# Eight-expert feed-forward: the last w2 load recut, the last result cut at column 320, three stores in halves

## The chip, the core and the metric

The kernel runs on one core of a Trainium2 chip. The metric is the device time of one execution in microseconds (us); lower is better. Engines that matter here: PE (TensorE, matrix products), ACT (ScalarE) and DVE (VectorE), which empty the accumulators, POOL (GpSimd), whose queue issues all weight loads, and SP (SyncE), whose queue issues most stores. Sixteen DMA engines carry all loads and stores of the core.

## What is computed

```python
n_experts, capacity, hidden, expert_hidden = 8, 256, 512, 2048
h = np.matmul(x, w1) + b1[:, np.newaxis, :]
h = np.maximum(h, 0)
return (np.matmul(h, w2) + b2[:, np.newaxis, :]).astype(np.float32)
```

All inputs and the output are float32 in HBM. An expert has a w1 of 512 x 2048 and a w2 of 2048 x 512, 4 MB each; the eight experts' weights are 64 MB of the 71.4 MB that are read. The output is 4 MB.

## The kernel before, in words

Weights and most of x are cast to float16 by the load itself, which POOL's queue issues (`load_w1` L69, `load_w2` L75, `load_x` L63). So a load reads 4 MB of float32 and writes 2 MB of float16 into SBUF. Products are float16 with float32 accumulators.

w2 of an expert is laid out as 128 partitions by 16 rows of 512 columns ("row" below means one of these 16; row j of every partition together is a contraction step of 128). Experts 0 to 5 load w2 whole, expert 6 in two halves of 8 rows, and the last, expert 7, in six pieces with a tile each (L85 to L91): rows 0-4, 4-8, 8-12, 12-14 with all columns, then rows 14-16 as two pieces of 256 columns. In one partition a piece of whole rows is one contiguous run, so one DMA packet; a piece of two rows by 256 columns is two packets of 512 B.

`first_product(e)` (L105) makes the hidden layer: 16 groups of 4 matmuls, each emptied by ACT with bias and ReLU (L117). Halfway it puts the next expert's transposes of x (L97). `second_product(e)` (L139) multiplies hidden by w2: it opens the accumulators with a matmul of the bias row (L151) and then walks the pieces of w2 in the order in which they are loaded (L163), 32 matmuls of 512 columns. Expert 7 has two column blocks, 0-256 and 256-512, with two accumulators each (one per 128 tokens), so 64 matmuls of 256 columns. When a block has its last row, `store` (L127) copies one accumulator by DVE (L130) and the other by ACT (L131) to SBUF and issues the store: from SP, one DMA of 512 KB for experts 0 to 6 (L137); for each block of expert 7 one DMA of 128 KB from SP (L134) and one from ACT (L135).

Steps run s = 0 to 10: first product of expert s, then second product of expert s - 3 (LAG). The order of instructions on PE and on POOL's queue is that of the program (`ordered`). POOL's order of loads is a list (L207 to L214): x, w1 and w2 in the order of use, w2 three experts behind w1. A load of POOL waits until its tile is free (three buffers each for w1 and w2; each piece of expert 7 has its own), and until the load eight places earlier on the queue has landed, because eight completion semaphores are used in turn.

Of the kernel before, what the change touches and what calls it, by code (L numbers as in the profile page):

```python
# [11 lines left out]
def kernel(  # L12
# [9 lines left out]
    nc = tc.nc  # L22
    fp32 = mybir.dt.float32
    fp16 = mybir.dt.float16
    E, T, H = x.shape
    M = w1.shape[2]
    P = 128
    nTB = T // P
    nKC = H // P
    nJ = M // P  # L30
    HH = H // 2
    LAG = 3
    nXF32 = 2

    def ordered(ins):
        return tc.keep_in_program_order(ins)

    singles = ctx.enter_context(tc.tile_pool(name="singles", bufs=1))
    w1_pool = ctx.enter_context(tc.tile_pool(name="w1", bufs=3))
    w2_pool = ctx.enter_context(tc.tile_pool(name="w2", bufs=3))  # L40
    w2t_pool = ctx.enter_context(tc.tile_pool(name="w2t", bufs=1))
    x_pool = ctx.enter_context(tc.tile_pool(name="xp", bufs=4))
    xT_pool = ctx.enter_context(tc.tile_pool(name="xTp", bufs=2))
    hT_pool = ctx.enter_context(tc.tile_pool(name="hT", bufs=LAG + 2))
    out_pool = ctx.enter_context(tc.tile_pool(name="outp", bufs=2))
    psum_x = ctx.enter_context(tc.tile_pool(name="psum_x", bufs=1, space=bass.MemoryType.PSUM))
    psum_h = ctx.enter_context(tc.tile_pool(name="psum_h", bufs=3, space=bass.MemoryType.PSUM))
    psum_o = ctx.enter_context(tc.tile_pool(name="psum_o", bufs=2, space=bass.MemoryType.PSUM))
# [10 lines left out]
    w1_sb = [None] * E  # L59
    w2_sb = [None] * E  # L60
# [14 lines left out]
    def load_w2(e):  # L75
        src = w2[e].rearrange("(p j) h -> p j h", j=nJ)
        w2_sb[e] = []
        if e < E - 1:
            t = w2_pool.tile([P, nJ, H], fp16, tag="w2", name="w2sb")
            step = nJ if e < E - 2 else nJ // 2  # L80
            for lo in range(0, nJ, step):
                ordered(nc.gpsimd.dma_start(out=t[:, lo : lo + step, :], in_=src[:, lo : lo + step, :]))  # L82
                w2_sb[e].append((lo, lo + step, 0, H, t[:, lo : lo + step, :]))
            return
        for lo, hi, c0, c1 in (  # L85
            (0, 4, 0, H), (4, 8, 0, H), (8, 12, 0, H), (12, 14, 0, H),
            (14, 16, 0, HH), (14, 16, HH, H),
        ):
            t = w2t_pool.tile([P, hi - lo, c1 - c0], fp16, tag=f"w2_{lo}_{c0}", name=f"w2_{lo}_{c0}")
            ordered(nc.gpsimd.dma_start(out=t, in_=src[:, lo:hi, c0:c1]))  # L90
            w2_sb[e].append((lo, hi, c0, c1, t))  # L91

    def transposes(e):
        pt = psum_x.tile([P, nKC, T], fp16, tag="psx", name="psx")
# [10 lines left out]
    def first_product(e):  # L105
        hT[e] = hT_pool.tile([P, nJ, T], fp16, tag="hT", name="hT")
        for j in range(nJ):
            ph = psum_h.tile([P, T], fp32, tag="ph", name="ph")
            for kc in range(nKC):
                ordered(nc.tensor.matmul(  # L110
                    out=ph,
                    lhsT=w1_sb[e][:, kc, :].rearrange("p (q j) -> p q j", j=nJ)[:, :, j],
                    rhs=xT[e][:, kc, :],
                    start=(kc == 0),
                    stop=(kc == nKC - 1),
                ))
            nc.scalar.activation(  # L117
                out=hT[e][:, j, :],
                in_=ph,
                func=mybir.ActivationFunctionType.Relu,  # L120
                bias=b1T[:, j, e : e + 1],
                scale=1.0,
            )
            if j == nJ // 2 and e + 1 < E:
                transposes(e + 1)

    def store(e, po, c0, c1, split):  # L127
        w = c1 - c0
        out_sb = out_pool.tile([P, nTB, w], fp32, tag=f"out{w}", name=f"out{w}")
        nc.vector.tensor_copy(out=out_sb[:, 0, :], in_=po[0])  # L130
        nc.scalar.copy(out=out_sb[:, 1, :], in_=po[1])  # L131
        dst = out[e].rearrange("(p tb) h -> p tb h", tb=nTB)[:, :, c0:c1]
        if split:
            nc.sync.dma_start(out=dst[:, 0, :], in_=out_sb[:, 0, :])  # L134
            nc.scalar.dma_start(out=dst[:, 1, :], in_=out_sb[:, 1, :])  # L135
        else:
            nc.sync.dma_start(out=dst, in_=out_sb)  # L137

    def second_product(e):  # L139
        if e < E - 1:  # L140
            blocks = [(0, H, psum_o, "po")]
        else:
            blocks = [(0, HH, psum_o, "po"), (HH, H, psum_h, "ph")]
        acc = {}
        for c0, c1, pool, tag in blocks:
            for tb in range(nTB):
                t = pool.tile(
                    [P, c1 - c0], fp32, tag=tag if tag == "ph" else f"{tag}{tb}", name=f"acc{tb}"
                )
                acc[c0, tb] = t  # L150
                ordered(nc.tensor.matmul(  # L151
                    out=t,
                    lhsT=ones1,
                    rhs=b2_sb[0:1, e * H + c0 : e * H + c1],
                    start=True,
                    stop=False,
                ))
        for lo, hi, p0, p1, t in w2_sb[e]:
            mine = [b for b in blocks if p0 <= b[0] and b[1] <= p1]
            for tb in range(nTB):  # L160
                for j in range(lo, hi):
                    for c0, c1, _, _ in mine:
                        ordered(nc.tensor.matmul(  # L163
                            out=acc[c0, tb],
                            lhsT=hT[e][:, j, tb * P : (tb + 1) * P],
                            rhs=t[:, j - lo, c0 - p0 : c1 - p0],
                            start=False,
                            stop=(j == nJ - 1),
                        ))
            if hi == nJ:  # L170
                for c0, c1, _, _ in mine:
                    store(e, [acc[c0, tb] for tb in range(nTB)], c0, c1, e == E - 1)

    x32 = singles.tile([P, nXF32, nTB, H], fp32)
    for e in range(nXF32):
# [4 lines left out]
        out=b2_sb,  # L180
        in_=b2.rearrange("e h -> (e h)").rearrange("(o f) -> o f", o=1),
# [10 lines left out]
    for j in range(nJ):  # L192
        for s in range(2):
            ordered(nc.tensor.matmul(  # L194
                out=pb[s * 64 : (s + 1) * 64, j, :, :],
# [5 lines left out]
    for s in range(2):  # L201
        nc.vector.tensor_copy(  # L202
            out=b1T[s * 64 : (s + 1) * 64, :, :], in_=pb[s * 64 : (s + 1) * 64, :, :, s]
        )
    transposes(0)

    loads = []  # L207
    for s in range(1, E + LAG):
        if s < E:
            if s >= nXF32:  # L210
                loads.append((load_x, s))
            loads.append((load_w1, s))
        if s >= LAG:
            loads.append((load_w2, s - LAG))  # L214
    n = 0

    def issue_until(done):
        nonlocal n
        while n < len(loads) and not done():
            loads[n][0](loads[n][1])  # L220
            n += 1

    for s in range(E + LAG):
        issue_until(lambda: (
            (min(s + 2, E - 1) < E and w1_sb[min(s + 2, E - 1)] is not None)
            and (s + 2 < LAG or w2_sb[min(s + 2 - LAG, E - 1)] is not None)
        ))
        if s < E:
            first_product(s)
        if s >= LAG:  # L230
            second_product(s - LAG)


# [28 lines left out]
```

## Time and profile before

| what | value |
|---|---|
| median of 5 runs | 185.97 us (185.74 to 186.18) |
| profiled execution, own time | 185.97 us |
| its span, first to last instruction | 184.0 us |
| PE busy | 139.4 us (76%) |
| ACT busy | 62.6 us (34%) |
| DVE busy | 13.3 us (7%) |
| POOL busy | 16.9 us (9%) |
| loads of POOL's queue (q0) | 35.14 MB as written, 91.3% of 16 engines' span |
| SP's queue (q1), first x load and most stores | 4.46 MB, 6.5% |
| ACT's queue (q10) | 0.85 MB, 1.3% |
| HBM | 71.39 MB read, 4.19 MB written |
| mean granted TensorE clock | 0.925 |

The profiled execution's time is 1.97 us above its span; that is what lies before the first and after the last instruction. MB of q0 count the bytes written into SBUF, which are half of those read. A DMA packet is one contiguous run on one of the 16 DMA engines; a 4-byte packet at the end of each DMA on each engine counts the completion.

### The profile page before, as it was taken

How to read it: one execution, taken by the hardware profiler on the slowest of the kernel's cores; microseconds unless marked ns; L12 is line 12 of the kernel's file. 1: busy time of each engine (PE TensorE's matmuls, PEld its weight loads, DVE VectorE, ACT ScalarE, POOL GpSimd, SP SyncE). 2: the span in 40 equal slices, each digit the busy share in tenths (PEclk: the TensorE clock that was granted, in tenths of full speed). 3: DMA queues.
4: the chain of work that ended last, by engine and by line, in shares of the span. 5: the costliest groups of instructions: out<-in, count | busy, mean ns of one | idle time of the engine just before them, and what ended most of it. 6: DMA issues, size and time to landing. Idle time of an engine off the chain costs nothing.

```text
span 184.0 us, 2209 instructions
## 1 busy us (share of the span) xinstructions
PE 139.4 (76%) x946; PEld 99.5 (54%) x946; DVE 13.3 (7%) x22; ACT 62.6 (34%) x138; POOL 16.9 (9%) x37
## 2 busy tenths in 40 slices
PE   0546989399631999619993499936999994999991
PEld 0535979379531745617473374735649741344680
DVE  0320101001000101001100101001010010010101
ACT  0022779449540421706045060441508701010101
POOL 7100030300300011100010000100006100100000
PEclk9999999969997599987999569996999999699999
DMA  5998999899998999899999999999999999999993
GB/s 184 286 214 187 228 228 224 176 227 228 230 221 178 228 228 228 162 284 209 199 228 233 259 207 214 228 252 229 203 228 228 228 232 220 248 232 226 247 216 114
DMA packets 6488, 40.57 MB, mean 220 GB/s; under 512 B 688, under 2 KB 1728, under 8 KB 4432
## 3 DMA queue, kind: packets, MB, share of 16 engines
q0 software_dynamic: 4320, 35.14, 91.3%
q1 hardware_dynamic: 1568, 4.46, 6.5%
q10 hardware_dynamic: 592, 0.85, 1.3%
q8 instruction: 7, 0.11, 0.2%
q14 instruction: 1, 0.01, 0.0%
HBM read 71.39 MB, written 4.19 MB: 411 GB/s over the span
## 4 chain that ended last, share of the span: by engine, by line
DMA 59%; PE 33%; another core or an unknown queue 3%; POOL 2%; issue 1%; ACT 0%; ACTq 0%; POOLq 0%
DMA x<-in_x_dram 25%; DMA w2sb<-in_w_dram 21%; PE acc L163 20%; DMA w1sb<-in_w_dram 12%; PE ph L110 11%; PE psx L97 1%; PE acc L151 1%; POOL w1sb L71 1%; ACT out L131 0%; POOL b_sb L179 0%; POOL w2sb L82 0%; POOL ident masks.py:199 0%; ACTq L135 0%; POOL ident masks.py:197 0%
## 5 line engine op out<-in xcount | busy, mean ns | idle before, releaser
L110 PE MATMUL ph<-xT,w1sb 128*128 128x256 f16 x512 | 68.6, 300 | 9.4 <-DMA w1sb<-in_w_dram 9.4
L117 ACT ACTIVATE hT<-ph,b1T 128x256 f16<-128x256 f32 x128 | 56.9, 474 | 46.6 <-PE ph L110 46.5
L110 PEld LDWEIGHTS <-w1sb 128*128 128x128 f16 x512 | 61.7, 149 | 15.7 <-DMA w1sb<-in_w_dram 10.4
L163 PE MATMUL acc<-w2sb,hT 128*128 128x512 f16 x224 | 51.2, 388 | 2.4 <-DMA w2sb<-in_w_dram 2.4
L163 PEld LDWEIGHTS <-hT 128*128 128x128 f16 x288 | 28.0, 99 | 32.7 <-issue 8.2
L131 ACT COPY out<-acc 128x512 f32<-128x512 f32 (+1 forms) x9 | 4.9, 541 | 60.7 <-PE acc L163 60.7
L97 PE MATMUL psx<-ident,x 128*128 128x128 f16 x64 | 7.0, 276 | 22.5 <-DMA x<-in_x_dram 21.8
L97 PEld LDWEIGHTS <-x 128*128 128x128 f16 x64 | 5.6, 131 | 23.5 <-DMA x<-in_x_dram 22.7
L103 DVE COPY xT<-psx 128x1024 f16<-128x1024 f16 x8 | 5.5, 691 | 84.6 <-PE psx L97 84.6
L130 DVE COPY out<-acc 128x512 f32<-128x512 f32 (+1 forms) x9 | 5.7, 632 | 73.9 <-PE acc L163 73.9
L71 POOL DMA_DIRECT2D w1sb<-in_w_dram x8 | 4.4, 554 | 68.6 <-PE ph L110 67.8
L82 POOL DMA_DIRECT2D w2sb<-in_w_dram x8 | 4.3, 536 | 57.1 <-PE acc L163 57.1
L194 PE MATMUL pb<-ident,b_rows 16*64 16x16 f32 x64 | 3.7, 266 | 6.6 <-DMA b_rows<-in_b_dram 6.6
L163 PE MATMUL acc<-w,hT 128*128 128x256 f16 x64 | 7.4, 273 | 0.1
L194 PEld LDWEIGHTS pb<-ident,b_rows 16*64 16x64 f32 x64 | 3.6, 198 | 6.5 <-issue 6.5
L117 ACT ACT_TABLE_LOAD x1 | 1.3, 1283 | 11.0 <-DVE b1T L202 11.0
L90 POOL DMA_DIRECT2D w<-in_w_dram x6 | 3.6, 613 | 13.5 <-DMA w2sb<-in_w_dram 13.5
L151 PE MATMUL acc<-b_sb,ones 1*128 1x512 f16 (+1 forms) x18 | 4.8, 355 | 0.0
L65 POOL DMA_DIRECT2D x<-in_x_dram x6 | 3.3, 546 | 0.6 <-DMA w1sb<-in_w_dram 0.6
L151 PEld LDWEIGHTS <-ones 1*128 1x128 f16 x18 | 1.1, 92 | 2.1 <-issue 2.1
L189 DVE CAST x<-x 128x1024 f16<-128x1024 f32 x2 | 1.4, 694 | 4.3 <-DMA x<-in_x_dram 4.3
L202 DVE COPY b1T<-pb 64x128 f32<-64x128 f32 x2 | 0.6, 288 | 3.7 <-PE pb L194 3.6
(8 smaller groups left out, 2.0 us busy)
## 6 DMA issues: line engine op xcount, KB each, us to landing
w1sb<-in_w_dram POOLq DMA_DIRECT2D x8, 2048.0 KB, 33.6
w2sb<-in_w_dram POOLq DMA_DIRECT2D x6, 2048.0 KB, 47.6
out_dram<-out SPq DMA_DIRECT2D x7, 512.0 KB, 10.3
w2sb<-in_w_dram POOLq DMA_DIRECT2D x2, 1024.0 KB, 25.4
x<-in_x_dram POOLq DMA_DIRECT2D x6, 256.0 KB, 40.2
w<-in_w_dram POOLq DMA_DIRECT2D x3, 512.0 KB, 32.9
x<-in_x_dram ACTq DMA_DIRECT2D x1, 512.0 KB, 5.2
x<-in_x_dram SPq DMA_DIRECT2D x1, 512.0 KB, 4.5
```

What stands on the lines that cost most here:

```text
L71: ordered(nc.gpsimd.dma_start(out=w1_sb[e], in_=w1[e].rearrange("(p kc) m -> p kc m", kc=nKC)))
L82: ordered(nc.gpsimd.dma_start(out=t[:, lo : lo + step, :], in_=src[:, lo : lo + step, :]))
L90: ordered(nc.gpsimd.dma_start(out=t, in_=src[:, lo:hi, c0:c1]))
L97: ordered(nc.tensor.transpose(out=pt[:, kc, tb * P : (tb + 1) * P], in_=x16[e][:, tb, :].rearrange("p (q kc) -> p q kc", kc=nKC)[:, :, kc] ...
L103: nc.vector.tensor_copy(out=xT[e], in_=pt)
L110: ordered(nc.tensor.matmul(out=ph, lhsT=w1_sb[e][:, kc, :].rearrange("p (q j) -> p q j", j=nJ)[:, :, j], rhs=xT[e][:, kc, :], start=(kc == 0),
L117: nc.scalar.activation(out=hT[e][:, j, :], in_=ph, func=mybir.ActivationFunctionType.Relu, bias=b1T[:, j, e : e + 1], scale=1.0,)
L130: nc.vector.tensor_copy(out=out_sb[:, 0, :], in_=po[0])
L131: nc.scalar.copy(out=out_sb[:, 1, :], in_=po[1])
L151: ordered(nc.tensor.matmul(out=t, lhsT=ones1, rhs=b2_sb[0:1, e * H + c0 : e * H + c1], start=True, stop=False,))
L163: ordered(nc.tensor.matmul(out=acc[c0, tb], lhsT=hT[e][:, j, tb * P : (tb + 1) * P], rhs=t[:, j - lo, c0 - p0 : c1 - p0], start=False, sto ...
L194: ordered(nc.tensor.matmul(out=pb[s * 64 : (s + 1) * 64, j, :, :], lhsT=b1_rows.rearrange("r (q j) -> r q j", j=nJ)[:, :, j], rhs=ident[0 ...
```

## The change

Four edits.

1. The last expert's w2 is loaded in eight pieces: 4, 3, 3 and 2 whole rows, then rows 12-14 and 14-16 with columns 0-320, then the same row pairs with columns 320-512. The new function `load_w2_piece` issues one of them.
2. The last expert's result is cut at column 320 where it was cut at 256. The 320-column block is stored by one DMA from SP that waits for both copies; the 192-column block as before by one DMA from SP and one from ACT. Both result tiles have a buffer of their own.
3. The stores of experts 0, 1 and 2 are issued as two DMAs of 64 partitions each.
4. The tiles of the 512-column results have three buffers where they had two. The list of loads is written with the step in which each is issued; the order on POOL's queue stays as it was up to the last expert's pieces.

```diff
-    HH = H // 2
+    HL = 320
     LAG = 3
+    PARTS = {0: 2, 1: 2, 2: 2}
...
-    out_pool = ctx.enter_context(tc.tile_pool(name="outp", bufs=2))
+    out_pool = ctx.enter_context(tc.tile_pool(name="outp", bufs=3))
...
-        for lo, hi, c0, c1 in (
-            (0, 4, 0, H), (4, 8, 0, H), (8, 12, 0, H), (12, 14, 0, H),
-            (14, 16, 0, HH), (14, 16, HH, H),
-        ):
-            t = w2t_pool.tile([P, hi - lo, c1 - c0], fp16, tag=f"w2_{lo}_{c0}", name=f"w2_{lo}_{c0}")
-            ordered(nc.gpsimd.dma_start(out=t, in_=src[:, lo:hi, c0:c1]))
-            w2_sb[e].append((lo, hi, c0, c1, t))
+    def load_w2_piece(e, lo, hi, c0, c1):
+        t = w2t_pool.tile([P, hi - lo, c1 - c0], fp16, tag=f"w2_{lo}_{c0}", name=f"w2_{lo}_{c0}")
+        src = w2[e].rearrange("(p j) h -> p j h", j=nJ)
+        ordered(nc.gpsimd.dma_start(out=t, in_=src[:, lo:hi, c0:c1]))
+        if w2_sb[e] is None:
+            w2_sb[e] = []
+        w2_sb[e].append((lo, hi, c0, c1, t))
...
-        out_sb = out_pool.tile([P, nTB, w], fp32, tag=f"out{w}", name=f"out{w}")
+        pool = out_pool if w == H else singles
+        out_sb = pool.tile([P, nTB, w], fp32, tag=f"out{c0}_{w}", name=f"out{w}")
...
-        if split:
+        if split and c1 == H:
             nc.sync.dma_start(out=dst[:, 0, :], in_=out_sb[:, 0, :])
             nc.scalar.dma_start(out=dst[:, 1, :], in_=out_sb[:, 1, :])
         else:
-            nc.sync.dma_start(out=dst, in_=out_sb)
+            step = P // PARTS.get(e, 1)
+            for lo in range(0, P, step):
+                nc.sync.dma_start(out=dst[lo : lo + step], in_=out_sb[lo : lo + step])
...
-            blocks = [(0, HH, psum_o, "po"), (HH, H, psum_h, "ph")]
+            blocks = [(0, HL, psum_o, "po"), (HL, H, psum_h, "ph")]
...
+    for piece in (
+        (0, 4, 0, H), (4, 7, 0, H), (7, 10, 0, H), (10, 12, 0, H),
+        (12, 14, 0, HL), (14, 16, 0, HL), (12, 14, HL, H), (14, 16, HL, H),
+    ):
+        ring.append((0, load_w2_piece, (E - 1,) + piece))
```

More of the change, by code (lines that the diff above doesn't have):

```diff
@@ L77, in load_w2 @@
         w2_sb[e] = []
[L78 to L84, printed above, removed]
-        for lo, hi, c0, c1 in (
-            (0, 4, 0, H), (4, 8, 0, H), (8, 12, 0, H), (12, 14, 0, H),
-            (14, 16, 0, HH), (14, 16, HH, H),
-        ):
-            t = w2t_pool.tile([P, hi - lo, c1 - c0], fp16, tag=f"w2_{lo}_{c0}", name=f"w2_{lo}_{c0}")
-            ordered(nc.gpsimd.dma_start(out=t, in_=src[:, lo:hi, c0:c1]))
-            w2_sb[e].append((lo, hi, c0, c1, t))
+        t = w2_pool.tile([P, nJ, H], fp16, tag="w2", name="w2sb")
+        step = nJ if e < E - 2 else nJ // 2
+        for lo in range(0, nJ, step):
+            ordered(nc.gpsimd.dma_start(out=t[:, lo : lo + step, :], in_=src[:, lo : lo + step, :]))
+            w2_sb[e].append((lo, lo + step, 0, H, t[:, lo : lo + step, :]))
+    def load_w2_piece(e, lo, hi, c0, c1):
[5 more added lines that the diff above has]
+        w2_sb[e].append((lo, hi, c0, c1, t))
     def transposes(e):
@@ L205 @@
     transposes(0)
-    loads = []
-    for s in range(1, E + LAG):
+    ring = []
+    for s in range(1, E + LAG - 1):
         if s < E:
             if s >= nXF32:
-                loads.append((load_x, s))
-            loads.append((load_w1, s))
+                ring.append((s - 2, load_x, (s,)))
+            ring.append((s - 2, load_w1, (s,)))
         if s >= LAG:
[L214 to L221, printed above, removed]
+            ring.append((s - 2, load_w2, (s - LAG,)))
+    for piece in (
[3 more added lines that the diff above has]
+        ring.append((0, load_w2_piece, (E - 1,) + piece))
     for s in range(E + LAG):
[L224 to L227, printed above, removed]
+        while ring and ring[0][0] <= s:
+            _, put, args = ring.pop(0)
+            put(*args)
         if s < E:
@@ L231 @@
             second_product(s - LAG)
+    assert not ring
 _INS = ['x', 'w1', 'w2', 'b1', 'b2']
```

## The prediction

> **What bounds the kernel now.** I read the page's slices first, then the queues, then the chain, then the last 12 us instruction by instruction and packet by packet.
>
> ```profile
> DMA  5998999899998999899999999999999999999993
> q0 software_dynamic: 4320, 35.14, 91.3%
> q1 hardware_dynamic: 1568, 4.46, 6.5%
> ```
>
> The DMA engines are busy in every slice from the second to the last but one. Loads and stores together take 99% of 16 engines' span. In the trace's packet records about 16 packets or more are under way in every microsecond from 5 to 177. So the load stream never runs dry, and its end can come earlier only by less DMA work.
>
> The second half of the chain of waits, and who waits for whom on POOL:
>
> ```profile
> 117.67 38.39 DMA w2sb<-in_w_dram
> 156.06 0.04 issue
> 156.10 8.75 PE acc L163 x32
> 164.85 0.53 PE acc L151 x2
> 165.38 7.01 PE acc L163 x32
> 172.40 0.54 PE acc L151 x4
> 172.94 6.77 PE acc L163 x60
> ...
> POOL w L90 <- DMA w2sb<-in_w_dram: 13.5, 2, 9.9
> ```
>
> From 156.10 PE works through the second products of experts 5, 6 and 7 almost without a gap. That looks like a PE-bound tail, but the landings say otherwise. By the completion counts in the trace the six pieces of expert 7 land at 169.78, 173.37, 175.79, 177.27, 179.05 and 179.71; PE starts the fifth at 179.10 and the sixth at 179.75, 0.1 and 0.2 us after it could have. PE and the load stream end within 0.3 us of each other, and the last landing decides by that little.
>
> The timeline of the last 5 us (start, length, engine, line):
>
> ```profile
> 178.77 1.58 PE L163 MATMUL acc<-w,hT 128*128 128x256 f16 x10
> 179.51 0.42 DVE L130 COPY out<-acc 128x256 f32<-128x256 f32 x1 [8.06 <-PE acc L163]
> 179.73 0.37 ACT L131 COPY out<-acc 128x256 f32<-128x256 f32 x1 [6.67 <-PE acc L163]
> 179.97 0.99 SPq L134 DMA_DIRECT2D out_dram<-out  x2
> 180.13 0.37 ACTq L135 DMA_DIRECT2D out_dram<-out  x1
> 180.17 0.42 DVE L130 COPY out<-acc 128x256 f32<-128x256 f32 x1 [0.23 <-PE acc L163]
> 180.55 0.37 ACT L131 COPY out<-acc 128x256 f32<-128x256 f32 x1 [0.44 <-PE acc L163]
> 180.95 0.35 ACTq L135 DMA_DIRECT2D out_dram<-out  x1
> ```
>
> ACT's second copy starts at 180.55 only because ACT was issuing the first block's store until 180.50; PE's last matmul ends at 180.35. The four stores' packets run from 180.80 to 182.47, and in that time the engines are full:
>
> ```profile
> DMA packets 576, 0.52 MB, mean 276 GB/s; under 512 B 64, under 2 KB 576, under 8 KB 576
> q10 hardware_dynamic: 288, 0.26, 41.9%
> q1 hardware_dynamic: 288, 0.26, 41.9%
> ```
>
> This is the DMA view of 180.7 to 182.6. So the very end is first store's issue (179.97) + 0.83 to its first packet + 1.67 for 512 KB; after 182.47 come 1.56 us of completion and closing. The later stores are hidden in the queue.
>
> **The change, part by part.**
>
> *Eight pieces instead of six.* The bytes are the same. On each DMA engine the pieces before are 3x8 + 8 + 2x16 = 64 packets; after they are 4x8 + 4x16 = 96. So 32 more packets. Load packets take 1227 ns at 16384 B, 624 at 8192, 324 at 4096, 173 at 2048 and 60 at 512. That is 22 ns + 0.0735 ns per byte. But packets overlap: in the last 0.7 us, when nothing else runs, the packets of one engine start every 41 ns (178.947, 178.988, 179.029), so a packet costs 41 - 37.6 = 3.4 ns beyond its bytes. I take this value, the row nearest in size and place: 32 x 3.4 = 0.11 us, and 0.02 for two more completions. Low end 0; high end, with no overlap, 32 x 22 = 0.70 us. The last landing moves from 179.71 to 179.84. No packet of 384 B is in the trace, and 512 B is the nearest row.
>
> The Trainium skill, "DMA: Bandwidth & Descriptors", Specifications, puts line rate at 512 B and more and says that below it the engine reads, modifies and writes. By that rule the 32 packets of 384 B would cost about twice 31.6 ns, and the sum would be about 0.6 us higher; no row here is short enough to show it.
>
> *Two more issues on POOL.* Each takes 0.55 to 0.72 us (line L90). By the turn of eight semaphores the seventh piece waits for the first half of expert 6's w2 (landed 161.94) and the eighth for the second half (167.15). Both are issued 9 us or more before the stream reaches them, with six pieces queued ahead. Nothing on POOL stands behind them. Cost 0. It would cost time only if the queue ran dry.
>
> *PE.* 64 matmuls before and after. A 256-column matmul starts every 109 ns; at 0.417 ns a column plus 2.5 ns, 320 columns take 136 and 192 take 82.5, the same 218 for a pair. PE reaches rows 12-14 after 48 of them, at 172.87 + 5.23 = 178.10, and ends that piece at 178.65. The second 320-column piece lands 32 x 31.6 ns + 0.02 = 1.03 us before the last one, so at 178.81; PE starts it at 178.85. The fourth 192-column group starts when the last piece lands, 179.88 (before: 179.75, +0.13).
>
> *First block's store.* From PE's start on the block's last piece to DVE's copy it was 0.42 us and to ACT's 0.64; with 64 more columns a matmul that is 0.47 and 0.74. The copies of 512 and 256 columns took 692 and 425 ns on DVE, 585 and 372 on ACT, so 320 columns take 0.49 and 0.43. DVE ends at 178.85 + 0.47 + 0.49 = 179.81, ACT at 180.02. SP's one DMA waits for the later, and is issued at 180.04 instead of 179.97: +0.07. Behind it SP holds only the 192-column store, due at 180.63.
>
> *Second block.* DVE copies from 180.25 to 180.61; SP issues at 180.63 (before 180.62). ACT has no issue in its way and copies from 180.41 for 0.32; its store is issued at 180.76 instead of 180.95, -0.19. This gain is covered: 512 KB still have to pass. Store packets took 47 ns at 1024 B and 166 at 4096, so 57 at 1280 and 37 at 768: 16x57 + 16x37 = 1.50 us an engine, as 32 x 47 = 1.50. The end is 180.04 + 0.83 + 1.67 = 182.54, against 182.47. Bounds: -0.19 if the last issue decides; +0.36 if a store of 256 rows starts as slowly as SP's first load of x did (issued 0.74, first packet 1.93: 1.19 where the stores need 0.83).
>
> *Three stores in halves.* SP issues three more DMAs of 0.33 us while it idles for tens of us; no copy waits for these stores. The packets stay the same 8 an engine of 159 to 172 ns, 166 in the mean. No store from 64 partitions is in the trace. Low end: all packets at 159 ns, 24 x 7 = -0.17 us. High end: each takes twice as long, 24 x 166 = +4.0 us. The nearest row of a narrow transfer is b_rows, 16 packets of 4096 B into 16 partitions: each took 159 ns with all within 0.35 us, no slower than the wide ones. I take 0.
>
> The Trainium skill, "SBUF — State Buffer", Door 1, says that the bandwidth of a DMA goes by how many of 16 ports its partitions reach, and the first 64 partitions reach eight. By that, two engines would share a port in these stores, and the sum would be up to 4.0 us higher; b_rows speaks against it, though for writes into SBUF alone.
>
> *Third result buffer, list of loads.* In the trace no copy waits for a store, and POOL's order is unchanged up to the pieces: 0.
>
> **Sum**, against the profiled execution's own 185.97 us, which is also the median of the five runs: +0.13 on the landing, of which +0.07 remains at the first store's issue, gives 186.0. A change of 0.2%, 0.37 us, is about what a measurement of this kernel can tell from none.
>
> **The rivals.**
>
> *A, as summed:* 186.0, own range 185.7 to 186.3. Chance 0.36.
>
> *B, half-stores hold the DMA engines longer* (the slower side). Two engines that read the same partitions' memory slow each other while both are in a store. In the window 77.3 to 81, while the first store runs, stores take 35% of the engines' time; 0.35 x 4.0 = 1.4 us. As the stream never idles, all of it arrives at the end: 187.4. It decides from a mean packet of 166 + 370/24 = 181 ns on. For it: nothing hides DMA work. Against: b_rows. Chance 0.24.
>
> *C, the 384-byte packets cost a double slot.* The last landing comes 1.0 us later, at 180.85; the second block's stores are issued at 181.65 and 181.77, their packets start 0.83 later and need 16 x 37 ns: 183.1, +0.6, so 186.6. Under 0.3 us of delay the first block's packets hide it. Chance 0.15.
>
> *D, the 256-row store starts late:* +0.07 + 0.36, 186.4. Chance 0.06.
>
> *E, faster.* The 16 engines end the load stream at different times, the mean one at 178.86 and the slowest at 179.42; the recut work can fall on them more evenly. Half of that lag gone is -0.28, and ACT's free queue deciding the end is -0.19: 185.5. For it: the last landing and ACT's late copy both sit on the chain. Against: nothing in the change balances the engines, and the final stores fill them, so the first issue decides. Chance 0.19.
>
> **How the numbers follow.** A is the likeliest, so 186.0. The range reaches from E's 185.5 to B's 187.4 and leaves out the far ends of both. Faster: 0.17 of E and 0.03 of A. Slower: 0.21 of B, 0.14 of C, 0.04 of D and 0.03 of A. The rest, 0.38, lies within 0.2%.
>
> **What would show it.** Right: the last piece lands near 179.85 from the same start, the 320-column store is issued near 180.0, its packets and the rest fill the engines for 1.6 to 1.7 us, ACT's store is issued 0.2 us earlier. B shows as packets of the first three stores over 181 ns or a whole stream that is late before 156. C shows as 384-byte packets over 40 ns apart. D shows as over 1 us from SP's issue to the first 1280-byte packet. The prediction is wrong if the stream reaches expert 7's pieces at another time than 167: then something upstream moved that I priced at nothing, such as a throttled stretch of PE's clock falling into the tail, where PE has only 0.3 us to spare.

## The result and the profile after

The changed kernel takes 186.51 us (median of 31 runs, 186.18 to 187.14) against 186.10 us for the kernel before, measured beside it (52 runs, 185.74 to 186.71). The ratio is 1.0024, 95% interval 1.0018 to 1.0030: slower by 0.4 us, a little more than the 0.2% that the prediction took for the least that can be told from none. The profiled execution has a span of 184.6 us against 184.0; its own time is 186.65 us, 0.14 above the median.

The page of the changed kernel, slices and queues:

```profile
DMA  5999999999999999899999999999999999999993
q0 software_dynamic: 4864, 35.14, 91.4%
q1 hardware_dynamic: 1744, 4.62, 6.8%
q10 hardware_dynamic: 448, 0.69, 1.0%
```

The load queue moves the same 35.14 MB in 544 more packets (512 of data: 32 on each of 16 engines; 32 that count completions). Its share is 91.4% of a longer span. The stream is as full as before.

The chain of waits from the same place as before:

```profile
117.30 38.95 DMA w2sb<-in_w_dram
156.25 0.28 issue
156.53 22.51 DMA w<-in_w_dram
179.04 0.04 issue
179.09 1.52 PE acc L166 x12
180.60 0.02 issue
180.62 0.32 ACT out L132
```

Now a load of expert 7 is the visible link from 156 to 179. That is no new wait of 22 us: before, PE and the stream ended within 0.3 us of each other, and now the stream is named. In this execution no stretch of half clock fell between 156 and 165 (granted clock 1.00 there, 0.81 in the profile before), so PE came to expert 7 at 171.49 instead of 172.87 and waited for its pieces. The timeline of the end, without weight loads:

```profile
178.22 0.70 PE L166 MATMUL acc<-w,hT 128*128 128x320 f16 x4 [0.39 <-DMA w<-in_w_dram]
179.09 1.50 PE L166 MATMUL acc<-w,hT 128*128 128x320 f16 x12 [0.16 <-DMA w<-in_w_dram]
179.56 0.49 DVE L131 COPY out<-acc 128x320 f32<-128x320 f32 x1 [9.48 <-PE acc L166]
179.82 0.42 ACT L132 COPY out<-acc 128x320 f32<-128x320 f32 x1 [8.14 <-PE acc L166]
180.28 0.59 SPq L140 DMA_DIRECT2D out_dram<-out  x1
180.46 0.36 DVE L131 COPY out<-acc 128x192 f32<-128x192 f32 x1 [0.41 <-PE acc L166]
180.62 0.32 ACT L132 COPY out<-acc 128x192 f32<-128x192 f32 x1 [0.38 <-PE acc L166]
180.96 0.56 SPq L135 DMA_DIRECT2D out_dram<-out  x1
180.97 0.37 ACTq L136 DMA_DIRECT2D out_dram<-out  x1
```

SP takes 0.59 us to issue the 320-column store, where a store's issue took 0.33 before, and its next one takes 0.56. The packet records add the decisive number: the first packet of that store starts at 181.53, 1.25 us after the issue. Before it was 0.83 (179.97 to 180.80). From there the engines are full, as before, in the DMA view of 181.5 to 183.2:

```profile
DMA packets 560, 0.52 MB, mean 309 GB/s; under 512 B 48, under 2 KB 560, under 8 KB 560
q1 hardware_dynamic: 416, 0.43, 72.8%
q10 hardware_dynamic: 144, 0.10, 17.5%
```

The last packet ends at 183.18 instead of 182.47. In parts: the issue is 0.31 us later, the wait for the first packet 0.42 longer, the packets take 1.65 instead of 1.67. Sum +0.71. But the span grew by 0.55 only: the last store counts as landed 0.48 us after its last packet instead of 0.53, and from there to the end it is 0.91 us instead of 1.02. The second difference turned out to be a lever of its own.

### The profile page after: what moved, and what is told of

Its sections match the earlier page's. It is cut to its first block, busy times and chain, and to the rows that moved or that the text cites. A ratio compares the mean times of both kernels' runs of the same rounds, so it can differ in the third digit from the quotient of the medians.

```text
span 184.6 us, 2210 instructions
## 1 busy us (share of the span) xinstructions
PE 138.1 (75%) x946; PEld 98.4 (53%) x946; DVE 13.3 (7%) x22; ACT 62.7 (34%) x138; POOL 18.3 (10%) x39
## 3 DMA queue, kind: packets, MB, share of 16 engines
q0 software_dynamic: 4864, 35.14, 91.4%
## 4 chain that ended last, share of the span: by engine, by line
DMA 71%; PE 21%; another core or an unknown queue 2%; POOL 2%; issue 1%; ACT 0%; POOLq 0%
DMA x<-in_x_dram 25%; DMA w2sb<-in_w_dram 21%; DMA w1sb<-in_w_dram 13%; DMA w<-in_w_dram 12%; PE ph L110 11%; PE acc L166 8%; PE psx L97 1%; PE acc L154 1%; POOL w1sb L72 1%; POOL b_sb L182 0%; POOL w2sb L82 0%; POOL ident masks.py:199 0%; POOL ident masks.py:197 0%; ACT out L132 0%
## 5 line engine op out<-in xcount | busy, mean ns | idle before, releaser
L166 PE MATMUL acc<-w2sb,hT 128*128 128x512 f16 x224 | 49.7, 379 | 1.3 <-DMA w2sb<-in_w_dram 1.3
L166 PEld LDWEIGHTS <-hT 128*128 128x128 f16 x288 | 27.2, 98 | 32.5 <-issue 6.5
L132 ACT COPY out<-acc 128x512 f32<-128x512 f32 (+2 forms) x9 | 4.9, 542 | 59.4 <-PE acc L166 59.4
L131 DVE COPY out<-acc 128x512 f32<-128x512 f32 (+2 forms) x9 | 5.7, 632 | 73.3 <-PE acc L166 73.3
L166 PE MATMUL acc<-w,hT 128*128 128x320 f16 (+1 forms) x64 | 7.9, 272 | 1.2 <-DMA w<-in_w_dram 1.0
L88 POOL DMA_DIRECT2D w<-in_w_dram x8 | 5.0, 635 | 22.2 <-DMA w2sb<-in_w_dram 22.2
L154 PE MATMUL acc<-b_sb,ones 1*128 1x512 f16 (+2 forms) x18 | 4.8, 355 | 0.0
```

Of the source, the lines that this page charges most:

```text
L154: ordered(nc.tensor.matmul(out=t, lhsT=ones1, rhs=b2_sb[0:1, e * H + c0 : e * H + c1], start=True, stop=False,))
L166: ordered(nc.tensor.matmul(out=acc[c0, tb], lhsT=hT[e][:, j, tb * P : (tb + 1) * P], rhs=t[:, j - lo, c0 - p0 : c1 - p0], start=False, sto ...
```

## The experiments

All times are medians; each run stands against the kernel before on the same chip, which gave 186.10, 186.07 and 186.10 us in the three groups. What is read from a trace comes from one execution of each kernel.

**First group: which part costs the time.** Four kernels, each with one part undone or done alone.

The changed kernel with the 320-column block stored by SP and ACT:

```diff
-        if split and c1 == H:
+        if split:
```

> The changed kernel with the 320-column block stored by one DMA from SP and one from ACT, as the 256-column block was. Theory 1 (the one DMA of 256 rows starts late: issue 180.28, first packet 181.53, 1.25 us, where the kernel before had 179.97 and 180.80, 0.83 us): SP issues after DVE's copy near 180.05, first packet near 180.9, last packet near 182.6 instead of 183.19, so 0.4 to 0.6 us less than the changed kernel, within 0.2 us of the kernel before. Theory 2 (the load stream ends 0.37 us later, 179.79 against 179.42, and that sets the end): no gain, 0.4 to 0.5 us above the kernel before. Both at work: in between, about 0.2 us above.

The changed kernel with whole stores throughout:

```diff
-    PARTS = {0: 2, 1: 2, 2: 2}
+    PARTS = {}
```

> The changed kernel with the first three stores whole again. Theory 1 (late start of the 256-row store): no difference, 0.4 to 0.5 us above the kernel before. Theory 3 (stores of 64 partitions hold the DMA engines longer, or their three extra DMAs do): the stream ends up to 0.3 us earlier and the time falls by as much. The packets of these stores took 170.4 to 170.9 ns in the mean in both traces, which speaks for no difference.

The kernel before with its first block in one store:

```diff
-        if split:
+        if split and c1 == H:
```

> The kernel before with its first 256-column block stored by one DMA of 256 rows from SP, nothing else changed. Theory 1: SP waits for both copies (issue 180.1 instead of 179.97) and the first packet follows 1.25 us later instead of 0.83; ACT's second copy is no longer late. The last packet goes from 182.47 to about 183.0: 0.4 to 0.6 us slower than the kernel before. Theory 2: no slower, or up to 0.2 us faster since ACT is free.

The kernel before with three stores in halves:

```diff
-            nc.sync.dma_start(out=dst, in_=out_sb)
+            step = P // (2 if e < 3 else 1)
+            for lo in range(0, P, step):
+                nc.sync.dma_start(out=dst[lo : lo + step], in_=out_sb[lo : lo + step])
```

> The kernel before with the first three stores in halves of 64 partitions, nothing else changed. Theory 1 and theory 2: no difference, within 0.15 us. Theory 3 (halves hold the engines): 0.2 to 0.4 us slower.

| kernel | us | ratio to before (95%) |
|---|---|---|
| changed, 320 block by SP and ACT | 186.24 | 1.0009 (1.0000 to 1.0017) |
| changed, no halves | 186.74 | 1.0032 (1.0019 to 1.0044) |
| before, first block in one store | 186.62 | 1.0031 (1.0019 to 1.0042) |
| before, three halves | 186.47 | 1.0014 (1.0006 to 1.0023) |

The one store alone makes the kernel before 0.52 us slower, as theory 1 has it. Its timeline shows the same signature as the changed kernel, with 256 columns:

```profile
179.78 0.37 ACT L131 COPY out<-acc 128x256 f32<-128x256 f32 x1 [6.68 <-PE acc L163]
180.17 0.60 SPq L137 DMA_DIRECT2D out_dram<-out  x1
180.88 0.55 SPq L134 DMA_DIRECT2D out_dram<-out  x1
```

Issue 180.17, 0.60 us long, first packet at 181.43: 1.25 us. The last load landed at 179.74, as in the kernel before (179.71), so theory 2 is out for this kernel. Taking the one store out of the changed kernel gains 0.27 us, less than theory 1's 0.4 to 0.6; why, the second group shows.

Two results fit no theory as a whole. Halves alone cost 0.37 us, as much as theory 3 says, but not in its way: their packets take 170.4 to 170.6 ns as ever and the last packet ends at 182.52 (before 182.47). And undoing halves in the changed kernel gains nothing; by the medians it costs 0.2, though the intervals overlap. The traces show where: what follows the last landing differs. SP closes the program by waiting for the eight completion counters of the SP and ACT queues in a fixed order, one wait every 0.06 us. In the run with SP and ACT (17 DMAs on these queues) the last store counts on the first of the eight, and seven waits come after it. From its instruction records (start, semaphores waited for):

```
182.775  107, 104   <- the last store's counter
182.837  109, 103
182.901  110, 102
182.963  114, 101
183.022  115, 100
183.084  116, 99
183.143  117, 108
183.204  118, 113
```

The view of SP's waits says the same: one long wait where the kernel before has four.

```profile
SPq L260 <- DMA out_dram<-out: 1.8, 1, 1.8
```

```profile
SPq L257 <- DMA out_dram<-out: 1.7, 4, 0.8
```

The first line is of the changed kernel with SP and ACT, the second of the kernel before (total us, times, longest).

**Second group: the counters.** The counters are used in turn, so the number of DMAs on the two queues decides which one the last store gets. Splitting one more or one less early store moves it.

```diff
-    PARTS = {0: 2, 1: 2, 2: 2}
+    PARTS = {0: 2, 1: 2}
```

on the changed kernel with SP and ACT (17 to 16 DMAs):

> The changed kernel with the 320-column block stored by SP and ACT, and only the first two stores in halves: 16 DMAs of the SP and ACT queues instead of 17. Theory 4: SP ends by waiting for the eight completion counters of those queues one after the other, about 0.06 us each, always in the same order; the last store of the 17-DMA kernel (186.24 us) counts on the first of them, so seven waits come after it, 0.43 us. With 16 DMAs the last store counts on the last counter, and the time is 0.35 to 0.45 us less: 185.8, 0.3 us below the kernel before. Theory 5 (the closing waits cost nothing; the time goes by the last packet): no change, 186.2.

The kernel before with two halves (`e < 2` where the earlier one had `e < 3`; 17 to 16):

> The kernel before with the first two stores in halves instead of none (14 to 16 DMAs). Theory 4: the last store counts on the last counter where it had two waits behind it in the kernel before, so 0.12 us less than before, 186.0; against three halves (17 DMAs, 186.47) 0.4 us less. Theory 3 (a half costs engine time): 0.15 to 0.25 us above the kernel before.

The changed kernel with `PARTS = {0: 2, 1: 2, 2: 2, 3: 2}` (16 to 17):

> The changed kernel with a fourth store in halves (16 to 17 DMAs), nothing else. Theory 4: the last store counts on the first counter, seven waits follow it: 0.35 to 0.45 us slower than the changed kernel, 186.9. Theory 3: 0.1 us slower. Theory 5: no change, 186.5.

Both DMAs of the 320-column block from SP:

```diff
-            nc.scalar.dma_start(out=dst[:, 1, :], in_=out_sb[:, 1, :])
+            (nc.scalar if c1 == H else nc.sync).dma_start(out=dst[:, 1, :], in_=out_sb[:, 1, :])
```

> As the run with SP and ACT and two stores in halves (16 DMAs), but both DMAs of the 320-column block from SP, so that ACT's second copy does not stand behind an issue. If the first issue and 512 KB of packets set the end: the same as that run within 0.1 us, 185.8. If the last issue sets it: ACT's store is issued 0.1 us earlier and the time falls by as much, 185.7.

| kernel | DMAs on SP and ACT | us | ratio (95%) | last landing to end, us |
|---|---|---|---|---|
| before | 14 | 186.10 | | 1.02 |
| before, one store | 13 | 186.62 | 1.0031 | 1.09 |
| changed, no halves | 13 | 186.74 | 1.0032 | 1.09 |
| changed | 16 | 186.51 | 1.0024 | 0.91 |
| before, two halves | 16 | 186.12 | 0.9995 (0.9987 to 1.0004) | 0.90 |
| changed, SP and ACT, two halves | 16 | 185.84 | 0.9990 (0.9981 to 0.9999) | 0.91 |
| changed, both from SP, two halves | 16 | 185.90 | 0.9994 (0.9985 to 1.0002) | 0.90 |
| before, three halves | 17 | 186.47 | 1.0014 | 1.33 |
| changed, SP and ACT, three halves | 17 | 186.24 | 1.0009 | 1.33 |
| changed, four halves | 17 | 186.84 | 1.0044 (1.0031 to 1.0057) | 1.33 |

The last column goes by the number of DMAs alone, over two kinds of kernels. One half more or less, from 16 to 17, changes the time by 0.33, 0.35 and 0.40 us in three pairs, where the traces have 0.42; in none of the three do the intervals overlap. Theory 4 stands, theories 3 and 5 fall. One forecast of theory 4 is not shown: from 14 to 16 DMAs it has 0.12 us less, and the two kernels before gave 186.10 and 186.12, with an interval that allows both 0.12 less and no change. So the halves' effect is not in the transfers: three of them happen to put the changed kernel's last store on the last counter.

The run with both DMAs from SP shows no gain from the free ACT beyond the interval, as expected where the first issue and the 512 KB behind it set the end.

The end of the fastest kernel, two halves and SP and ACT:

```profile
179.30 0.49 DVE L131 COPY out<-acc 128x320 f32<-128x320 f32 x1 [9.05 <-PE acc L166]
179.57 0.43 ACT L132 COPY out<-acc 128x320 f32<-128x320 f32 x1 [7.71 <-PE acc L166]
179.82 1.15 SPq L135 DMA_DIRECT2D out_dram<-out  x2
180.03 0.37 ACTq L136 DMA_DIRECT2D out_dram<-out  x1
180.44 0.32 ACT L132 COPY out<-acc 128x192 f32<-128x192 f32 x1 [0.44 <-PE acc L166]
180.79 0.35 ACTq L136 DMA_DIRECT2D out_dram<-out  x1
```

SP's first issue waits for DVE only: 179.82, with its first packet 0.83 later at 180.65 and the last packet at 182.32. It is 0.67 us faster than the changed kernel with the same number of DMAs (which has one more half beside the one store), and 0.1% faster than the kernel before.

**Third group: why the one store starts late, and what the recut is worth.** Both kernels before with the recut or the cut alone have two halves, so 16 DMAs.

```diff
-    PARTS = {0: 2, 1: 2, 2: 2}
+    PARTS = {0: 2, 1: 2, 7: 2}
```

> The changed kernel with the 320-column block stored by two DMAs from SP, one for each 64 partitions (128 rows each), and the first two stores in halves: 16 DMAs as in the changed kernel, the last store on the last counter. Both DMAs still wait for both copies. Theory 6 (the late first packet belongs to the 256 rows of one DMA): first packet 0.83 us after the issue near 180.1, so the packets end 0.3 to 0.4 us earlier and the time is 186.1 to 186.2. Theory 7 (the wait for both copies and the place on SP cost the time, not the rows): no better than the changed kernel, 186.5.

```diff
-            (0, 4, 0, H), (4, 8, 0, H), (8, 12, 0, H), (12, 14, 0, H),
-            (14, 16, 0, HH), (14, 16, HH, H),
+            (0, 4, 0, H), (4, 7, 0, H), (7, 10, 0, H), (10, 12, 0, H),
+            (12, 14, 0, HH), (14, 16, 0, HH), (12, 14, HH, H), (14, 16, HH, H),
```

> The kernel before with eight pieces (4, 3, 3, 2 rows, then two pairs by columns 0-256 and two by 256-512), stores as before, first two stores in halves: 16 DMAs. Against the 16-DMA kernel before (186.12): the first block's last piece lands about 1.2 us before the last landing instead of 0.7, so its store can start 0.3 to 0.5 us earlier, if the first issue sets the end; 24 to 32 more packets cost 0.1. Then 185.8 to 186.0. If only the last landing counts: 186.2.

```diff
-    HH = H // 2
+    HH = 320
```

> The kernel before with its six pieces and the cut at column 320 instead of 256, stores by SP and ACT, first two stores in halves: 16 DMAs. Against the 16-DMA kernel before (186.12): the last piece is smaller, so the first block's last piece lands 0.1 us later before the end and its two more columns' worth of copies take 0.07 longer, while the second block's stores are shorter. If the first issue sets the end: 186.1 to 186.3. If the last issue sets it: 185.9.

The 320-column block in two DMAs of 64 partitions gave 186.81 us, ratio 1.0039 (1.0026 to 1.0053): no faster than the changed kernel, and by the medians 0.3 us slower. Its end:

```profile
179.68 0.42 ACT L132 COPY out<-acc 128x320 f32<-128x320 f32 x1 [6.69 <-PE acc L166]
180.13 1.21 SPq L140 DMA_DIRECT2D out_dram<-out  x2
180.72 0.37 ACTq L136 DMA_DIRECT2D out_dram<-out  x1
181.44 0.57 SPq L135 DMA_DIRECT2D out_dram<-out  x1
```

Each of its DMAs has 128 rows, as a plain store has, and still takes 0.57 to 0.60 us to issue; the first packet comes 1.22 us after the issue. So it is not the number of rows, and theory 6 falls. Theory 7 forecast the time's direction, but the wait for both copies is not the whole either, since the late first packet comes after the issue. What these slow stores share is the shape: both accumulators' parts of a partition in one DMA, runs of 1280 B (1024 in the kernel before) that lie apart in HBM; the trace lists it as [1,128] and [1,256] where the plain ones have [128,1]. The length of the run is not it: plain stores of 1280 B start 0.83 us after their issue too. Whether the shape as such costs the time, and why, was not tried. A long issue alone is no mark of that shape: SP took 0.47 to 0.60 us for each plain half of the first stores ([64,1]) as well, against 0.33 to 0.36 for whole ones. Of the 0.42 us in the changed kernel, 0.26 are the longer issue and 0.16 come after it.

This run showed one thing more. Its 1280-byte packets took 85.7 ns in the mean, against 58.3 from 128 partitions. The Trainium skill ("SBUF — State Buffer", Door 1) has the rule that the first 64 partitions reach half of the ports. Here the stores of 64 partitions run together without loads and their packets take 1.47 times as long, which points the same way; that the ports are the cause is not shown. In the middle of the load stream, in the halves of the first stores, packets stayed at 170.4 to 170.9 ns.

The recut at 256 gave 185.99 (0.9993, 0.9984 to 1.0003), the cut at 320 with six pieces 186.15 (1.0003, 0.9994 to 1.0011), against 186.12 with neither and 185.84 with both, all with 16 DMAs and 0.90 to 0.91 us from the last landing to the end. Both lie in the ranges forecast for the case that the first issue sets the end. The intervals overlap. That recut and cut together gain some 0.1 us (by the ratios) to 0.3 (by the medians) is likely, and how it divides is not settled. In the recut kernel at 256 the first issue is early (179.54), but ACT's last is late (181.05), and its last packet ends at 182.62, so there the last issue sets the end; at 320 both come out together.

The traces show one thing that the recut changes. In the two six-piece kernels with 16 DMAs the piece of rows 12-14 with all columns landed late, at 178.56 (cut at 256) and 178.45 (cut at 320). PE had to do its 8 matmuls before the 4 that finish the first block, so the first store waited for PE. Lines of the six-piece kernel cut at 256, then of the eight-piece kernel cut at 256:

```profile
178.60 1.91 PE L165 MATMUL acc<-w,hT 128*128 128x256 f16 x16 [0.51 <-DMA w<-in_w_dram]
180.34 0.81 SPq L134 DMA_DIRECT2D out_dram<-out  x2
```

```profile
179.54 1.68 SPq L134 DMA_DIRECT2D out_dram<-out  x2
181.05 0.35 ACTq L135 DMA_DIRECT2D out_dram<-out  x1
```

With six pieces the first issue is at 180.34 and 180.36; with eight pieces, plain stores and 16 DMAs it is at 179.54, 179.82 and 179.91. But in the profile of the kernel before that piece landed at 177.27, and the issue came at 179.97. That execution had the stretch of half clock between 156 and 165 (0.81, against 1.00 in the two kernels with the late piece), and its store of expert 6 was issued at 173.09 instead of 171.83 and 171.89. So what the recut is worth seems to differ from one execution to the next; whether that store is what delays the piece was not tried.

## Why the prediction was right, and where it was not

The sum gave 186.0, the measured time is 186.51: inside the range of 185.5 to 187.4, on the side that had the larger chance (slower, 0.42), but beyond the likeliest case's own range of 185.7 to 186.3. That it is inside is luck in good part. The upper bound came from rival B, and 0.35 of the 0.42 from B and C, which both fell; the case that came true, D, had 0.04 of it. Point by point:

- *The load stream.* Right. Packets of 384 B start every 32 ns on an engine and those of 640 B every 50 to 51, where 31.6 and 50.4 were worked out. The Trainium skill's rule of 512 B ("DMA: Bandwidth & Descriptors", Specifications) did not show in these casting loads, which read 768 B for each 384 B that they write, and rival C falls with it; the doubling was the prediction's own, the page names no factor. The last load was to land at 179.84. In this profile it landed at 180.06, but that is one execution's scatter: in six other kernels with the changed pieces (SP and ACT with three and with two halves, both from SP, no halves, four halves, 64-partition stores) it landed at 179.76, 179.85, 179.74, 179.84, 179.89 and 179.81, 179.82 in the mean. The five kernels with six pieces (before, one store, three halves, two halves, cut at 320) landed theirs at 179.71, 179.74, 179.56, 179.84 and 179.73, 179.72 in the mean. So the recut costs 0.10 us on the landing, where 0.13 was worked out.
- *Two more issues on POOL.* Right: the last two were issued at 162.12 and 167.65, as expert 6's halves landed, and the piece landed 12 us after the later one.
- *PE.* Right: pairs of 136 and 82 ns (178.355 to 178.490, 180.098 to 180.180), no bound.
- *First block's store.* From PE's start on the last piece to SP's issue it took 1.19 us, as worked out (178.85 to 180.04). Here the step failed that followed: "180.04 + 0.83 + 1.67". The 0.83 belongs to a plain store; this one took 1.25. The bound beside it, +0.36 from SP's first load of x, had the place and nearly the size (0.42), but got a chance of 0.06 as rival D, for which the prediction gives no reason; and it went by the 256 rows, where a DMA of 128 rows started as late (1.22). The nearest row in shape was the load of x, with two runs a partition; the plain store was nearest in time only. D gave 186.4, 0.1 us from the median.
- *Halves.* Right that their packets cost nothing (rival B falls: 170.4 to 170.9 ns, as the first three stores had before; the 166 of the prediction is the mean of the last store alone), wrong that they have no effect. SP took 0.47 to 0.60 us to issue each half, where 0.33 was counted; it idled meanwhile, so this cost nothing that shows. The term missing from the sum is the closing: I took 1.56 us from last packet to end as a constant. By traces, last landing to end is 0.91 us with 16 DMAs and 1.02 with 14, so the changed kernel had a gain of 0.11 that offset part of the late store.
- *ACT's earlier issue, -0.19.* It did not come: ACT's store went at 180.97 against 180.95, since PE's last group came 0.2 us later in this execution. In the runs with no halves and with four halves, which have the same one store, it is issued at 180.76 and 180.81, as forecast, and they are no faster than the changed kernel. Covered, as argued.

Put together by the runs: the one store +0.67 us (186.51 against 185.84 at 16 DMAs; 0.52 alone on the kernel before, with the closing of 13 DMAs), recut and cut together -0.28 by the medians (185.84 against 186.12) and -0.1 by the ratios, and the step from 14 to 16 DMAs +0.02 by the medians (186.12 against 186.10) and -0.1 by ratio and traces.

## What to carry to other kernels

Where the last stores fill the DMA engines, the first store's start counts, not the number of issues saved: one DMA that waits for two copies and gathers two runs a partition sent its first packet 0.42 us later after its issue than a plain one that follows its own copy. Price a new DMA by the row with the same shape, not by the one that is nearest in time. When an early edit changes the end by a few tenths of a microsecond, look at the closing waits before looking for a cause in the transfers.

## What was not expected of the hardware

- The program's end waits for the completion counters in a fixed order, 0.06 us each. Which counter the last store gets is decided by how many DMAs were issued on the SP and ACT queues: 0.90 to 0.91 us from the last landing to the end with 16, 1.02 with 14, 1.09 with 13, 1.33 with 17.
- A store of two runs a partition takes SP 0.57 to 0.61 us to issue and starts 1.22 to 1.26 us after, against 0.33 and 0.83; SP's next store is issued in 0.54 to 0.58 too. Plain halves of 64 partitions took 0.47 to 0.60 us to issue.
- Stores of 64 partitions without loads beside them: 85.7 ns for a packet of 1280 B, against 58.3.
